# Narrower score windows in a neighbourhood-attention block: 23, 31 and 24 key columns, and value rows loaded in small pieces

## The chip, the cores and the metric

The kernel runs on one core of one Trainium2 chip. Its time is the device time of one execution in microseconds; the time before is the median of three runs. The engines are TensorE (PE, with PEld for its weight loads), VectorE (DVE), ScalarE (ACT), GpSimd (POOL) and SyncE (SP), whose only work here is to issue transfers. ACT issues a few transfers too.

## The reference

One encoder layer over 1024 tokens of 1024 channels. The normalised input goes through one projection. Half of its columns feed a gated convolution over 31 positions, the other half an attention with 8 heads of 64 channels. Both outputs are joined, projected and added to the input; then a gated feed-forward layer follows. The change touches the attention alone:

```
qg = q.reshape(B, rows, GRID_W, H, Dh)        # 16 rows of 64 tokens
col_start = jnp.clip(cols - kw // 2, 0, GRID_W - kw)      # kw = 16
row_start = jnp.clip(r - kh // 2, 0, rows - kh)           # kh = 8
s = jnp.einsum("bqhd,brqchd->bhqrc", q_r, k_win) * scale
s = s + bias                                   # learned, by 2-D offset
p = jax.nn.softmax(s, axis=(-2, -1))
out = jnp.einsum("bhqrc,brqchd->bqhd", p, v_win)
```

A query at row r and column c of the 16 by 64 grid sees 8 rows and 16 columns of keys around it, clamped to the grid.

## The kernel before, in words

The queries are cut in 8 tiles of 128: two halves of the grid's rows (`rh`, 8 rows each) by four blocks of 16 columns (`cb`). For a tile the kernel computes scores against a rectangle of keys that covers all its queries' windows, and a table of biases holds -1e30 where a query may not look. The rectangle has `AR` = 12 rows and, from `WIN`, 24, 32, 32 or 24 columns: 288 or 384 keys. `order` (line 667) takes the column blocks 0, 3, 1, 2, each with both halves: eight stages. A stage has four pairs of heads, numbered `i` = 0 to 31 over all stages.

For a pair: `score_mm` (line 680) makes two products of 64 rows by the rectangle; `score_max` (693) adds the table and finds the largest on DVE; `score_exp` (698) exponentiates on ACT and sums; `score_norm` (709) divides on POOL. `flip` (720) transposes the probabilities on PE in three groups of four key rows (96 or 128 keys each), `flip_out` (727 on DVE for even pairs, 729 on ACT for odd ones) copies them back, and `weigh` (739) multiplies them by the values, summing over three groups. Even pairs put scores and transposes into the same two PSUM banks (`cv`), one after the other.

The order of the work is written out by hand: engines run their instructions in the order of the program. The loop at line 880 takes two pairs a turn: scores of `i` and `i+1`, transposes of `i-3` and `i-2`, weighing of `i-5` and `i-4`. Before it, the value projection of tokens (`value`, eight steps of 128 tokens) is interleaved with the first pairs. `value_out` (447) stores each step's values to DRAM on ACT's queue.

Values come back from DRAM by `load_vw` (660) on SP's queue: for a window, tiles of two groups, a group being four grid rows; one load per grid row of the four, so a group lies as 4 x 24 or 4 x 32 rows of a tile, and two groups may come in one load. `load_vw(0, 0, 1)` and `load_vw(0, 2)` follow the seventh value step, `load_vw(0, 3)`, `load_window(3)` and a table the eighth; windows 1 and 2 are loaded in the loop. `table` (647) loads a stage's biases, made in DRAM far earlier by `bias_tables` (lines 510 to 527) with many small transfers, which share SP's queue with the weights' loads (149).

Tiles named G, ST, H are taken from rings of buffers; the framework places the waits. A transfer signals its landing by one of eight semaphores, dealt in turn over the transfers of both queues.

Of the kernel before, what the change touches and what calls it, by code (L numbers as in the profile page):

```python
# [6 lines left out]
F32 = mybir.dt.float32  # L7
# [5 lines left out]
P = 128  # L13
# [4 lines left out]
NH = 8  # L18
HD = 64
# [3 lines left out]
EPS = 1e-6  # L23
NEG = -1e30
GW = 64
AR = 12
SIDE = (16, 17, 18, 19, 20, 21, 22)
WIN = ((0, 24, 8), (8, 32, 0), (24, 32, 0), (40, 24, 0))


def layout(v):
# [39 lines left out]
def build(ctx, tc, a):  # L71
    nc = tc.nc
    pe, act, dve, pool = nc.tensor, nc.scalar, nc.vector, nc.gpsimd
# [45 lines left out]
    def lr(w):  # L119
        return w[:, :512], w[:, 512:]  # L120
# [127 lines left out]
    ident = T("ident", [P, P], 1, "ident")  # L248
# [24 lines left out]
    for _ in range(9):  # L273
# [4 lines left out]
    t1 = [dr.tile([NH, 16, 15, ncol], F32, name=f"t1{ty}") for ty, ncol in enumerate((24, 32, 24))]  # L278
    tf = {(rh, ty): dr.tile([16, 8, NH, AR * t1[ty].shape[-1]], F32, name=f"tf{rh}{ty}")
          for rh in range(2) for ty in range(3)}  # L280

    def rstd_of(ss, scale, name):
# [159 lines left out]
    vd = dr.tile([S, 512], F32, name="vd")  # L442
# [57 lines left out]


    aside_dma = []

    def bias_tables():
        neg = G("neg")
        pool.memset(neg, NEG)

        def fill1(ty):
            n = 15 * t1[ty].shape[-1]
            nc.sync.dma_start(t1[ty].rearrange("h j u b -> (h j) (u b)"), neg[:, :n])  # L510

        def fill2(rh, ty):
            n = 3 * AR * t1[ty].shape[-1] if ty != 1 else 2 * AR * 32
            for o in range(0, NH * AR * t1[ty].shape[-1], n):
                w = min(n, NH * AR * t1[ty].shape[-1] - o)
                nc.sync.dma_start(tf[rh, ty].rearrange("j i h c -> (j i) (h c)")[:, o:o + w], neg[:, :w])

        def run(ty, j):
            b0, shift = ((max(j - 8, 0), 15), (j, 7), (min(j, 8), 7))[ty]
            o = b0 - j + shift  # L520
            nc.sync.dma_start(t1[ty][:, j, :, b0:b0 + 16], a["rpb"][:, :, o:o + 16])

        def rows_of(rh, ty, i):
            ncol = t1[ty].shape[-1]
            a0 = max(i - 4, 0) if rh == 0 else min(i, 4)
            u0 = a0 - i + (7 if rh == 0 else 3)
            nc.sync.dma_start(tf[rh, ty][:, i, :, a0 * ncol:(a0 + 8) * ncol],
                              t1[ty][:, :, u0:u0 + 8, :].rearrange("h j u b -> j h (u b)"))
        for ty in (0, 2, 1):
            fill1(ty)  # L530
        for ty in (0, 2, 1):
            aside_dma.extend(lambda ty=ty, j=j: run(ty, j) for j in range(16))
            for rh in range(2):
                aside_dma.append(lambda rh=rh, ty=ty: fill2(rh, ty))
        for ty in (0, 2, 1):
            for rh in range(2):
                aside_dma.extend(lambda rh=rh, ty=ty, i=i: rows_of(rh, ty, i) for i in range(8))
# [30 lines left out]
    for kp in range(4):  # L568
        parts = []
# [66 lines left out]


    def table(rh, ty):
        n = AR * t1[ty].shape[-1]
        src = tf[rh, ty].rearrange("j i h c -> (j i) (h c)")  # L640
        if rh == 0 and ty == 0:
            parts = [(G(f"tab{k}")[:, :n * min(3, NH - 3 * k)], 3 * k) for k in range(3)]
        else:
            parts = [(H(f"tab{rh}{ty}")[:, :NH * n], 0)]
        heads = []
        for w, h0 in parts:
            nc.sync.dma_start(w, src[:, h0 * n:h0 * n + w.shape[-1]])
            heads += [w[:, o:o + n] for o in range(0, w.shape[-1], n)]
        return heads


    vwt, vw = {}, {}

    def load_vw(cb, *gs):
        c0, ncol, _ = WIN[cb]
        if gs[0] % 2 == 0:
            vwt[cb, gs[0] // 2] = G(f"vw{cb}{gs[0]}").rearrange("p (g d) -> p g d", d=512)
        w = vwt[cb, gs[0] // 2]
        for r in range(4):
            nc.sync.dma_start(w[r * ncol:(r + 1) * ncol, gs[0] % 2:gs[-1] % 2 + 1, :],  # L660
                              vd.rearrange("(g r c) d -> r c g d", r=4, c=GW)[r, c0:c0 + ncol, gs[0]:gs[-1] + 1, :])
        for g in gs:
            vw[cb, g] = w[:4 * ncol, g % 2, :]
# [5 lines left out]
    at = []  # L669

    def score_mm(i):
        s_, hp = divmod(i, 4)
        rh, cb = order[s_]
        t = rh * 4 + cb
        c0, ncol, _ = WIN[cb]
        s2 = cv(f"s{i}") if i > 0 and i % 2 == 0 else None
        out = []
        for hh in range(2):
            s = (mm(f"s{i}{hh}") if s2 is None else lr(s2)[hh])[:, :AR * ncol]
            pe.matmul(s, qT[hh * HD:(hh + 1) * HD, hp, t * P:(t + 1) * P],  # L680
                      k4[hh * HD:(hh + 1) * HD, hp, rh * 4:rh * 4 + AR, c0:c0 + ncol], start=True, stop=True)
# [28 lines left out]


    def flip(i):
        s_, hp = divmod(i, 4)
        m = 4 * WIN[order[s_][1]][1]
        if i % 2 == 0:
            cvs[i] = cv(f"p{i}")
        pp[i] = lr(cvs[i]) if i % 2 == 0 else [mm(f"p{i}{hh}") for hh in range(2)]
        for hh, pt in enumerate(pp[i]):
            for g in range(3):
                pe.transpose(pt[:m, g * P:(g + 1) * P], es[i][:, hh, g * m:(g + 1) * m], ident)  # L720

    def flip_out(i, hh=None):
        m = 4 * WIN[order[i // 4][1]][1]
        w = et[i][:m, :, :384]
        pTs[i] = [w[:, h].rearrange("p (n q) -> p n q", q=P) for h in range(2)]
        if hh is None:
            dve.tensor_copy(w, cvs[i].rearrange("p (h n) -> p h n", h=2)[:m, :, :384])
        else:
            act.copy(w[:, hh], pp[i][hh][:m, :384])

    def weigh(i):
        s_, hp = divmod(i, 4)
        rh, cb = order[s_]
        if hp == 0:
            os_[s_] = tp(f"o{s_}").rearrange("p (c q) -> p c q", c=4)
        for g in range(3):
            for hh in range(2):
                c = (2 * hp + hh) * HD
                pe.matmul(os_[s_][hh * HD:(hh + 1) * HD, hp], vw[cb, rh + g][:, c:c + HD], pTs[i][hh][:, g],  # L739
                          start=g == 0, stop=g == 2)  # L740

    def half(name):
        w = H(name, F32R).rearrange("p (w k s) -> p w k s", w=2, s=512)
# [21 lines left out]
    def load_window(cb):  # L765
        load_vw(cb, 0, 1)
        load_vw(cb, 2, 3)
# [112 lines left out]
    for i in range(4, 32, 2):  # L880
# [24 lines left out]
        if i > 4:  # L905
            weigh(i - 5)
# [541 lines left out]
    def quarter(w, o, t):  # L1448
        return w[:, o + t * 512:o + t * 512 + 512]
# [32 lines left out]
    for s, p in enumerate(SEQ):  # L1482
        for k in range(QF - 2):
            n = s * QF + k
# [23 lines left out]
    for half in range(2):  # L1508
# [4 lines left out]
        w = quarter(om["u"], 0, 3)[:, part_]  # L1513
# [17 lines left out]
```

## Time and profile before

| | us |
|---|---|
| median of three runs (1035.32 to 1035.88) | 1035.74 |
| the profiled execution | 1035.18 |
| its span, first to last instruction | 1033.5 |
| PE busy in the span | 1024.3 |
| DVE busy | 782.3 |
| ACT busy | 478.7 |
| POOL busy | 436.0 |
| attention loop, first scores to last weighing of the loop | 235.6 to 295.1 |
| TensorE clock granted | 1.0 throughout |

A row of the timeline gives start and length in us from the span's start, the engine (a q behind it means its queue or sequencer), the line of the kernel, what it writes and reads, the shapes, and how many instructions are merged in the row; in brackets stands the engine's idle time before it and what ended that. A wait row gives who waited for whom, the total in us, how often, and the longest. Matmul lengths overlap the next one's start, so times between starts are the ones to use.

### The profile page before, as it was taken

The page shows a single profiled execution, that of the slowest core. Times are in us where ns is not written, and L with a number is a line of the kernel's source. Part 1 is how long each engine was busy: PE and PEld are TensorE (multiplying, and loading weights), DVE is VectorE, ACT ScalarE, POOL GpSimd, SP SyncE. Part 2 cuts the span into 40 slices and gives each one's busy share as a digit, 9 for nine tenths or more (in the row PEclk, how much of TensorE's full clock was granted, in tenths as well). Part 3 has the DMA queues.
Part 4 walks back from the last instruction along what each step waited for, and adds up shares of the span by engine and source line. Part 5 has one row for each costly group of instructions (what it writes and reads, how often), then busy time and mean ns, then how long its engine had stood idle before and what let it go on. Part 6 is the DMA issues. An engine that isn't in the chain of part 4 may idle for free.

```text
span 1033.5 us, 15158 instructions
## 1 busy us (share of the span) xinstructions
PE 1024.3 (99%) x5334; PEld 853.8 (83%) x5334; DVE 782.3 (76%) x1234; ACT 478.7 (46%) x1045; POOL 436.0 (42%) x345
## 2 busy tenths in 40 slices
PE   9999999999999999999999999999999999999998
PEld 7888888877787788877888888888888888888887
DVE  5788997896755376998787787787787767758874
ACT  7565348836866345523334334343342443433432
POOL 1036764524641345047776667567566200003210
PEclk9999999999999999999999999999999999999999
DMA  9426781337403621122434424434441696633631
GB/s 347 165 79 201 225 255 53 122 115 234 124 22 122 235 92 41 47 107 89 156 119 157 139 96 153 153 101 145 144 143 71 222 365 238 224 102 123 214 122 42
DMA packets 75084, 152.53 MB, mean 148 GB/s; under 512 B 13824, under 2 KB 22784, under 8 KB 74368
## 3 DMA queue, kind: packets, MB, share of 16 engines
q1 hardware_dynamic: 72992, 148.21, 42.5%
q10 hardware_dynamic: 2016, 3.36, 0.9%
q8 instruction: 42, 0.69, 0.3%
q14 instruction: 34, 0.28, 0.1%
HBM read 112.38 MB, written 44.76 MB: 152 GB/s over the span
## 4 chain that ended last, share of the span: by engine, by line
PE 93%; DVE 5%; ACT 1%; issue 1%; DMA 0%; ACTq 0%; DVEq 0%
PE B L115 5%; PE B L116 5%; PE B L117 5%; PE z L115 4%; PE z L117 4%; PE z L116 4%; PE D L115 3%; PE D L116 3%; PE D L117 3%; PE gl L117 3%; PE gl L116 3%; PE gl L115 3%; PE pj L115 3%; PE pj L116 3%; PE pj L117 3%; PE p L720 2%
## 5 line engine op out<-in xcount | busy, mean ns | idle before, releaser
L363 DVE SCALAR_TENSOR_TENSOR cv<-u,par,cv 128x1009 f32<-128x1009 f32 (+14 forms) x92 | 117.4, 1277 | 2.3
L389 POOL TENSOR_TENSOR pa<-pa,pr 128x1022 f32<-128x1022 f32 (+5 forms) x24 | 58.0, 2417 | 48.7 <-ACT pr L388 36.1
L107 ACT CAST op<-sr 128x512 fp32r<-128x512 f32 x77 | 47.7, 619 | 57.7 <-PE B2d L117 26.7
L1474 POOL TENSOR_TENSOR ou<-ou,resm 128x512 f32<-128x512 f32 x8 | 12.0, 1506 | 139.8 <-DVE ou L1465 126.1
L111 DVE TENSOR_TENSOR op<-sr,op 128x512 fp32r<-128x512 f32 x77 | 57.6, 748 | 16.5 <-ACT op L107 16.4
L709 POOL TENSOR_SCALAR e<-e,rs 128x288 f32<-128x288 f32 (+1 forms) x64 | 33.9, 545 | 41.8 <-DVE rs L707 40.1
L1024 DVE TENSOR_TENSOR ts<-gu,ts 128x512 f32<-128x512 f32 x40 | 46.3, 1158 | 0.7
L107 ACT CAST op<-wd 128x512 fp32r<-128x512 f32 x54 | 33.4, 619 | 28.5 <-DVE wd L1370 18.0
L698 ACT ACTIVATE e<-e,mx 128x288 f32<-128x288 f32 (+1 forms) x64 | 36.5, 572 | 18.8 <-DVE mx L693 16.9
L111 DVE TENSOR_TENSOR op<-wd,op 128x512 fp32r<-128x512 f32 x54 | 39.8, 738 | 1.7 <-ACT op L107 0.6
L693 DVE CUSTOM_DVE_ANT_0 e<-s,tab 128x288 f32<-128x288 f32 (+1 forms) x64 | 28.7, 503 | 13.6 <-PE s L680 13.6
L980 POOL TENSOR_TENSOR sq<-sq,sq 128x512 f32<-128x512 f32 x12 | 17.1, 1423 | 51.6 <-ACT sq L976 51.4
L1283 DVE TENSOR_TENSOR g<-D,g 128x512 f32<-128x512 f32 x22 | 15.2, 690 | 23.4 <-PE D L117 23.4
L416 ACT ACTIVATE sq<-z,r 128x64 f32<-128x64 f32 x96 | 28.3, 329 | 5.2 <-PE z L117 5.2
L1260 ACT ACTIVATE D<-D 128x512 f32<-128x512 f32 x22 | 12.8, 582 | 32.6 <-DVE D L1259 32.6
L388 ACT ACTIVATE pr<-u,par 128x1022 f32<-128x1022 f32 (+5 forms) x24 | 27.0, 1138 | 1.6 <-ACT vs L446 1.2
L720 PEld LDWEIGHTS p<-ident,e 128*96 128x96 f32 (+1 forms) x192 | 20.5, 133 | 6.8 <-POOL e L709 6.3
L115 PE MATMUL B2d<-op 128*128 128x512 f32 x66 | 25.8, 391 | 0.0
L117 PE MATMUL B2d<-op 128*128 128x512 f32 x66 | 25.7, 389 | 0.0
L116 PE MATMUL B2d<-op 128*128 128x512 f32 x66 | 25.7, 389 | 0.0
L739 PE MATMUL o<-e,vw 96*64 96x128 f32 (+1 forms) x384 | 24.7, 277 | 0.0
L720 PE MATMUL p<-ident,e 128*96 128x128 f32 (+1 forms) x192 | 24.4, 276 | 0.0
(1454 smaller groups left out, 3734.5 us busy)
## 6 DMA issues: line engine op xcount, KB each, us to landing
gu<-in_gu SPq DMA_DIRECT2D x44, 512.0 KB
sr<-sd SPq DMA_DIRECT2D x77, 256.0 KB
sd<-sd SPq DMA_DIRECT2D x22, 512.0 KB
wd<-in_wd SPq DMA_DIRECT2D x36, 256.0 KB
sd<-g SPq DMA_DIRECT2D x33, 256.0 KB
x<-in_x SPq DMA_DIRECT2D x8, 512.0 KB
xT<-in_xp SPq DMA_DIRECT2D x8, 512.0 KB
xd<-xT SPq DMA_DIRECT2D x16, 256.0 KB
```

Of the source, the lines that this page charges most:

```text
L107: act.copy(hi, src)
L111: eng.tensor_tensor(*[w[..., sl] for w in (lo, src, hi.bitcast(F32))], OP.subtract)
L115: pe.matmul(acc, lh, rh, start=start, stop=False, skip_group_check=True)
L116: pe.matmul(acc, lh, rl, start=False, stop=False, skip_group_check=True)
L117: pe.matmul(acc, ll, rh, start=False, stop=stop, skip_group_check=True)
L363: dve.scalar_tensor_tensor(acc[:, o], uc[:, i], dwk[:, c, t:t + 1], acc[:, o], OP.mult, OP.add)
L389: pool.tensor_tensor(pa[:, o], pa[:, o], pr[:, o], OP.add)
L693: dve.tensor_tensor_reduce(out=es[i][:, hh], in0=s[hh], in1=tab[rh, cb][2 * hp + hh], scale=-1.0, scalar=3.0e38, op0=OP.add, op1=OP.min, a ...
L698: act.activation(e, e, AF.Exp, bias=mx.pop((i, hh)), scale=-1.0, accum_out=sums[i][:, hh:hh + 1])
L709: pool.tensor_scalar(es[i][:, hh], es[i][:, hh], rs[:, hh:hh + 1], 1.0, op0=OP.mult, op1=OP.mult)
L720: pe.transpose(pt[:m, g * P:(g + 1) * P], es[i][:, hh, g * m:(g + 1) * m], ident)
L1024: dve.tensor_tensor(o, l, r, OP.subtract)
```

## The change

The rectangle of keys is cut to what some query of the tile may see: 11 rows for the upper half, 12 for the lower; 23, 31, 31 and 24 columns. The eight stages are then 253, 276, 264, 288, 341, 372, 341 and 372 keys wide. `groups` cuts a stage's keys in groups: of 128 for the first stage, so there are two, and of four grid rows for the others, so there are three. `whole` rounds a group's rows up to a multiple of 32; a transpose then takes a few of the next group's keys with it, and behind the last group POOL zeroes the columns up to the end. The value tiles get rows of zeros in the same places, loaded from a small zero array `zd` in DRAM, which `bias_tables` fills with one store.

Values of the first stage get a tile of their own, `load_first`, in which the 253 keys lie one behind the other. `value_rows` loads a run of rows whole if its length is a multiple of 8, and in pieces of up to 16 otherwise. So a group of the windows with 23 or 31 columns takes 9 loads (8 pieces and the zero rows) instead of 4, the first stage's tile 23, and windows with 24 columns stay at 4. The tables of the first stage lie in two buffers instead of three, and the table `table(1, 2)` is loaded ahead of the values of window 3 instead of behind them.

```
-AR = 12
+AR = (11, 12)
-WIN = ((0, 24, 8), (8, 32, 0), (24, 32, 0), (40, 24, 0))
+WIN = ((0, 23), (8, 31), (24, 31), (40, 24))
+NCOL = (23, 31, 24)
...
+    zd = dr.tile([4, 2, 512], F32, name="zd")
     def bias_tables():
         neg = G("neg")
         pool.memset(neg, NEG)
+        zero = ST("zero")[:8]
+        pool.memset(zero, 0.0)
+        nc.sync.dma_start(zd.rearrange("p g d -> (p g) d"), zero)
...
+            parts = [(G(f"tab{k}")[:, :4 * n], 4 * k) for k in range(2)]
-            parts = [(G(f"tab{k}")[:, :n * min(3, NH - 3 * k)], 3 * k) for k in range(3)]
...
+    def value_rows(w, at_, g, src, n):
+        m = n if n % 8 == 0 else 16
+        for o in range(0, n, m):
+            e = min(n, o + m)
+            nc.sync.dma_start(w[at_ + o:at_ + e, g, :], src[o:e])
+
+    def whole(n):
+        return -(-n // 32) * 32
+
     def load_vw(cb, *gs):
...
         for r in range(4):
-            nc.sync.dma_start(w[r * ncol:(r + 1) * ncol, gs[0] % 2:gs[-1] % 2 + 1, :],
-                              vd.rearrange("(g r c) d -> r c g d", r=4, c=GW)[r, c0:c0 + ncol, gs[0]:gs[-1] + 1, :])
+            value_rows(w, r * ncol, slice(gs[0] % 2, gs[-1] % 2 + 1), v4[r, c0:c0 + ncol, gs[0]:gs[-1] + 1, :], ncol)
+        n = whole(4 * ncol)
+        if n > 4 * ncol:
+            nc.sync.dma_start(w[4 * ncol:n, gs[0] % 2:gs[-1] % 2 + 1, :], zd[:n - 4 * ncol, :len(gs), :])
+    def load_first():
+        c0, ncol = WIN[0]
+        w = vwt["first"] = G("vwf").rearrange("p (g d) -> p g d", d=512)
+        for r in range(AR[0]):
+            for g in range(2):
+                a0, a1 = max(r * ncol, g * P), min((r + 1) * ncol, g * P + P)
+                if a0 < a1:
+                    t = r * GW + c0 + a0 - r * ncol
+                    value_rows(w, a0 - g * P, g, vd[t:t + a1 - a0, :], a1 - a0)
+        n = AR[0] * ncol - P
+        nc.sync.dma_start(w[n:whole(n), 1, :], zd[:whole(n) - n, 0, :])
...
+    def groups(s_):
+        n, m = width(s_), P if s_ == 0 else 4 * WIN[order[s_][1]][1]
+        return [slice(o, min(o + m, n)) for o in range(0, n, m)]
...
-            es[i] = et[i][:, :, :AR * WIN[cb][1]]
+            n, gs = width(s_), groups(s_)
+            es[i] = et[i][:, :, :n]
+            end = gs[-1].start + whole(gs[0].stop)
+            if n < end:
+                pool.memset(et[i][:, :, n:end], 0.0)
...
-            for g in range(3):
-                pe.transpose(pt[:m, g * P:(g + 1) * P], es[i][:, hh, g * m:(g + 1) * m], ident)
+            gs = groups(i // 4)
+            m = whole(gs[0].stop)
+            for g, k in enumerate(gs):
+                pe.transpose(pt[:m, g * P:(g + 1) * P], et[i][:, hh, k.start:k.start + m], ident)
...
-                pe.matmul(os_[s_][hh * HD:(hh + 1) * HD, hp], vw[cb, rh + g][:, c:c + HD], pTs[i][hh][:, g],
-                          start=g == 0, stop=g == 2)
+                pe.matmul(os_[s_][hh * HD:(hh + 1) * HD, hp], v[:n, c:c + HD], pTs[i][hh][:n, g],
+                          start=g == 0, stop=g == len(gs) - 1)
...
     value(6)
-    load_vw(0, 0, 1)
+    load_first()
+    load_vw(0, 1)
     load_vw(0, 2)
...
     load_vw(0, 3)
+    tab[1, 3] = table(1, 2)
     load_window(3)
-    tab[1, 3] = table(1, 2)
```

More of the change, by code (lines that the diff above doesn't have):

```diff
@@ L277, in build @@
     qgs = T("qgs", [P, 1], 1, "qgs")
-    t1 = [dr.tile([NH, 16, 15, ncol], F32, name=f"t1{ty}") for ty, ncol in enumerate((24, 32, 24))]
-    tf = {(rh, ty): dr.tile([16, 8, NH, AR * t1[ty].shape[-1]], F32, name=f"tf{rh}{ty}")
+    t1 = [dr.tile([NH, 16, 15, ncol], F32, name=f"t1{ty}") for ty, ncol in enumerate(NCOL)]
+    tf = {(rh, ty): dr.tile([16, 8, NH, AR[rh] * NCOL[ty]], F32, name=f"tf{rh}{ty}")
           for rh in range(2) for ty in range(3)}
@@ L506, in bias_tables @@
         pool.memset(neg, NEG)
+        zero = ST("zero")[:8]
+        pool.memset(zero, 0.0)
+        nc.sync.dma_start(zd.rearrange("p g d -> (p g) d"), zero)
         def fill1(ty):
-            n = 15 * t1[ty].shape[-1]
+            n = 15 * NCOL[ty]
             nc.sync.dma_start(t1[ty].rearrange("h j u b -> (h j) (u b)"), neg[:, :n])
         def fill2(rh, ty):
-            n = 3 * AR * t1[ty].shape[-1] if ty != 1 else 2 * AR * 32
-            for o in range(0, NH * AR * t1[ty].shape[-1], n):
-                w = min(n, NH * AR * t1[ty].shape[-1] - o)
+            n = (3 if ty != 1 else 2) * AR[rh] * NCOL[ty]
+            for o in range(0, NH * AR[rh] * NCOL[ty], n):
+                w = min(n, NH * AR[rh] * NCOL[ty] - o)
                 nc.sync.dma_start(tf[rh, ty].rearrange("j i h c -> (j i) (h c)")[:, o:o + w], neg[:, :w])
@@ L523, in rows_of @@
         def rows_of(rh, ty, i):
-            ncol = t1[ty].shape[-1]
+            ncol = NCOL[ty]
             a0 = max(i - 4, 0) if rh == 0 else min(i, 4)
@@ L652, in build @@
     vwt, vw = {}, {}
+    def value_rows(w, at_, g, src, n):
[5 more added lines that the diff above has]
+        return -(-n // 32) * 32
     def load_vw(cb, *gs):
-        c0, ncol, _ = WIN[cb]
-        if gs[0] % 2 == 0:
+        c0, ncol = WIN[cb]
+        if (cb, gs[0] // 2) not in vwt:
             vwt[cb, gs[0] // 2] = G(f"vw{cb}{gs[0]}").rearrange("p (g d) -> p g d", d=512)
         w = vwt[cb, gs[0] // 2]
+        v4 = vd.rearrange("(g r c) d -> r c g d", r=4, c=GW)
         for r in range(4):
-            nc.sync.dma_start(w[r * ncol:(r + 1) * ncol, gs[0] % 2:gs[-1] % 2 + 1, :],
-                              vd.rearrange("(g r c) d -> r c g d", r=4, c=GW)[r, c0:c0 + ncol, gs[0]:gs[-1] + 1, :])
+            value_rows(w, r * ncol, slice(gs[0] % 2, gs[-1] % 2 + 1), v4[r, c0:c0 + ncol, gs[0]:gs[-1] + 1, :], ncol)
+        n = whole(4 * ncol)
+        if n > 4 * ncol:
+            nc.sync.dma_start(w[4 * ncol:n, gs[0] % 2:gs[-1] % 2 + 1, :], zd[:n - 4 * ncol, :len(gs), :])
         for g in gs:
-            vw[cb, g] = w[:4 * ncol, g % 2, :]
+            vw[cb, g] = w[:, g % 2, :]
+    def load_first():
[9 more added lines that the diff above has]
+        nc.sync.dma_start(w[n:whole(n), 1, :], zd[:whole(n) - n, 0, :])
     k4 = kT.rearrange("p c (r w) -> p c r w", w=GW)
@@ L669, in build, with width @@
     at = []
+    def width(s_):
+        rh, cb = order[s_]
+        return AR[rh] * WIN[cb][1]
+    def groups(s_):
+        n, m = width(s_), P if s_ == 0 else 4 * WIN[order[s_][1]][1]
+        return [slice(o, min(o + m, n)) for o in range(0, n, m)]
     def score_mm(i):
@@ L674, in score_mm @@
         t = rh * 4 + cb
-        c0, ncol, _ = WIN[cb]
+        c0, ncol = WIN[cb]
         s2 = cv(f"s{i}") if i > 0 and i % 2 == 0 else None
@@ L678, in score_mm @@
         for hh in range(2):
-            s = (mm(f"s{i}{hh}") if s2 is None else lr(s2)[hh])[:, :AR * ncol]
+            s = (mm(f"s{i}{hh}") if s2 is None else lr(s2)[hh])[:, :width(s_)]
             pe.matmul(s, qT[hh * HD:(hh + 1) * HD, hp, t * P:(t + 1) * P],
-                      k4[hh * HD:(hh + 1) * HD, hp, rh * 4:rh * 4 + AR, c0:c0 + ncol], start=True, stop=True)
+                      k4[hh * HD:(hh + 1) * HD, hp, rh * 4:rh * 4 + AR[rh], c0:c0 + ncol], start=True, stop=True)
             out.append(s)
@@ L712, in flip @@
     def flip(i):
-        s_, hp = divmod(i, 4)
-        m = 4 * WIN[order[s_][1]][1]
         if i % 2 == 0:
@@ L718, in flip @@
         for hh, pt in enumerate(pp[i]):
-            for g in range(3):
-                pe.transpose(pt[:m, g * P:(g + 1) * P], es[i][:, hh, g * m:(g + 1) * m], ident)
+            gs = groups(i // 4)
+            m = whole(gs[0].stop)
+            for g, k in enumerate(gs):
+                pe.transpose(pt[:m, g * P:(g + 1) * P], et[i][:, hh, k.start:k.start + m], ident)
     def flip_out(i, hh=None):
-        m = 4 * WIN[order[i // 4][1]][1]
-        w = et[i][:m, :, :384]
+        gs = groups(i // 4)
+        m, n = whole(gs[0].stop), len(gs) * P
+        w = et[i][:m, :, :n]
         pTs[i] = [w[:, h].rearrange("p (n q) -> p n q", q=P) for h in range(2)]
         if hh is None:
-            dve.tensor_copy(w, cvs[i].rearrange("p (h n) -> p h n", h=2)[:m, :, :384])
+            dve.tensor_copy(w, cvs[i].rearrange("p (h n) -> p h n", h=2)[:m, :, :n])
         else:
-            act.copy(w[:, hh], pp[i][hh][:m, :384])
+            act.copy(w[:, hh], pp[i][hh][:m, :n])
     def weigh(i):
@@ L735, in weigh @@
             os_[s_] = tp(f"o{s_}").rearrange("p (c q) -> p c q", c=4)
-        for g in range(3):
+        gs = groups(s_)
+        for g, k in enumerate(gs):
+            n = whole(k.stop - k.start)
+            v = vwt["first"][:, g, :] if s_ == 0 else vw[cb, rh + g]
             for hh in range(2):
                 c = (2 * hp + hh) * HD
-                pe.matmul(os_[s_][hh * HD:(hh + 1) * HD, hp], vw[cb, rh + g][:, c:c + HD], pTs[i][hh][:, g],
-                          start=g == 0, stop=g == 2)
+                pe.matmul(os_[s_][hh * HD:(hh + 1) * HD, hp], v[:n, c:c + HD], pTs[i][hh][:n, g],
+                          start=g == 0, stop=g == len(gs) - 1)
     def half(name):
```

2 lines of the change are left out of this document (1 added, 1 removed).

## The prediction

> **What bounds the kernel now.** I read the page first: the busy shares and the chain that ended last. The columns of the first row are busy time, share and instructions.
>
> ```profile
> PE 1024.3 (99%) x5334; PEld 853.8 (83%) x5334; DVE 782.3 (76%) x1234; ACT 478.7 (46%) x1045; POOL 436.0 (42%) x345
> ...
> PE 93%; DVE 5%; ACT 1%; issue 1%; DMA 0%; ACTq 0%; DVEq 0%
> ```
>
> PE sets the end, but an average over 1033.5 us says nothing of the attention stage that the change edits. So I took the timeline of PE there; columns are start, length, engine, line, and in brackets the idle time before and what ended it. An fp32 product is two entries, a transpose is one.
>
> ```profile
> 235.64 1.24 PE L680 MATMUL s<-kT,qT 64*128 64x288 f32 x8
> 236.82 1.51 PE L720 MATMUL p<-ident,e 128*96 128x128 f32 x12
> 238.26 0.88 PE L739 MATMUL o<-e,vw 96*64 96x128 f32 x12
> 239.45 1.24 PE L680 MATMUL s<-kT,qT 64*128 64x288 f32 x8 [0.31 <-DVE e L727]
> ...
> 243.52 1.24 PE L680 MATMUL s<-kT,qT 64*128 64x288 f32 x8
> 244.69 1.52 PE L720 MATMUL p<-ident,e 128*96 128x128 f32 x12
> 246.14 1.53 PE L739 MATMUL o<-e,vw 96*64 96x128 f32 x24
> 247.60 1.24 PE L680 MATMUL s<-kT,qT 64*128 64x288 f32 x8
> ...
> 251.68 1.24 PE L680 MATMUL s<-kT,qT 64*128 64x288 f32 x8
> ...
> 259.83 1.56 PE L680 MATMUL s<-kT,qT 64*128 64x384 f32 x8
> 261.33 1.51 PE L720 MATMUL p<-ident,e 128*96 128x128 f32 x12
> ...
> 274.54 1.53 PE L720 MATMUL p<-ident,e 128*128 128x128 f32 x12
> 275.99 1.53 PE L739 MATMUL o<-e,vw 128*64 128x128 f32 x24
> 277.45 1.56 PE L680 MATMUL s<-kT,qT 64*128 64x384 f32 x8
> ```
>
> One turn of the loop (two pairs of heads) is scores, transposes, weighing, then the next scores with no gap: 243.52 to 247.60 is 4.08 us of PE and nothing else. Only the first turn shows a gap, 0.31 us before 239.45, for the copy of line 727 that frees the two banks which scores and transposes share. That gap says how near the second limit is: 3.81 us from 235.64 to 239.45 is the shortest turn which that copy allows, 0.27 under 4.08. So PE time saved here is worth its full size only for the first quarter of a microsecond in a turn.
>
> **What the change saves on PE.** Key columns fall from 24 to 23 and 32 to 31, rows from 12 to 11 for the upper half of the queries. Widths of the eight stages in their order: 288, 288, 288, 288, 384, 384, 384, 384 become 253, 276, 264, 288, 341, 372, 341, 372: 35+12+24+0+43+12+43+12 = 181 columns, times 8 heads = 1448. The score block of four products starts the transposes 1.17 us later at 288 columns (243.52 to 244.69) and 1.50 at 384 (259.83 to 261.33): 0.33 us for 4x96 columns, 0.86 ns each. 1448 x 0.86 ns = 1.24 us.
>
> [...]
>
> The first stage, 253 wide, is cut in two groups of 128 and 125 instead of three of 96: one transpose and one weighing product fewer for each of 8 heads. A transpose costs 1.45/12 = 0.121 us (244.69 to 246.14): 8 x 0.121 = 0.97. A weighing product costs 1.46/12 = 0.122 (246.14 to 247.60): 0.97. The groups elsewhere stay three, their sums still run over 96 or 128 rows, so the padding to 32 costs PE nothing: with 128 rows the transposes take 1.45 us (274.54 to 275.99) and the weighing 1.46 (to 277.45), as with 96. Together 3.18 us; in the first two turns the copy's limit gives back about 0.3 (the second turn's PE work falls by 0.77, its limit by about 0.5). **PE: -2.85 us.** Of this 2.05 lies before the fifth pair's weighing, which matters below.
>
> **What it adds off PE, at no cost.** 28 memsets on POOL that zero the ends of the probabilities. Nearest row and the work beside it:
>
> ```profile
> L384 POOL MEMSET pa<- x4: 98/114/123, 33.3 to 182.6; 128x1 f32 x4
> ...
> 59.88 0.96 POOL L506 MEMSET neg<- 128x1024 f32 x1
> ...
> 242.02 0.98 POOL L709 TENSOR_SCALAR e<-e,rs 128x288 f32<-128x288 f32 x2 [1.41 <-DVE rs L707]
> ```
>
> Two a turn at 0.12 us, up to 0.2 for 35 columns, stand ahead of the normalisation in POOL's queue, and POOL idles 1.41 us there waiting for DVE. If that cover went, at most 0.4 us a turn. DVE and ACT get less work (fewer columns); neither sets the turn after the second. A zero tile and its store join SP's queue ahead of the bias fills, which start right after the 0.96 us memset: half a memset (0.5) and an issue (0.4) push all that follows by 0.9 us. The nearest user is the last weight of the query projection:
>
> ```profile
> 140.08 2.85 POOL L111 TENSOR_TENSOR w03l<-w03r,w03h 128x1024 fp32r<-128x1024 f32 x1
> ...
> 144.91 0.39 PE L116 MATMUL z<-w03l,hT 128*128 128x512 f32 x1
> ```
>
> It is ready at 142.93 and wanted at 144.91: 2.0 us of slack against 0.9. Nothing. The tables of the bias shrink a little. More waits stand in PE's queue at the weighing (more loads per tile); the present ones leave no gap at 246.14, so I take 0.
>
> **The value loads.** This part decides. Before, the values of the first window come in 12 loads; now the first stage's own tile takes 23 (22 pieces of 7 to 16 rows and a row of zeros), and three more groups 9 each: 50. Call the stores of value tokens (line 447, on ACT's queue) t0 to t7. First SP's queue and ACT's stores:
>
> ```profile
> 210.13 0.75 SPq L660 DMA_DIRECT2D vw<-vd  x2
> 217.59 0.71 SPq L660 DMA_DIRECT2D vw<-vd  x2
> 229.68 0.29 SPq L660 DMA_DIRECT2D vw<-vd  x1
> 230.01 1.50 SPq L660 DMA_DIRECT2D vw<-vd  x3
> 238.52 1.53 SPq L660 DMA_DIRECT2D vw<-vd  x4
> 239.68 2.85 SPq L660 DMA_DIRECT2D vw<-vd  x7
> 242.57 1.30 SPq L647 DMA_DIRECT2D tab<-tf  x3
> ...
> 227.66 0.33 ACTq L447 DMA_DIRECT2D vd<-vs  x1
> 228.76 0.33 ACTq L447 DMA_DIRECT2D vd<-vs  x1
> 236.47 0.33 ACTq L447 DMA_DIRECT2D vd<-vs  x1
> ```
>
> The store t5 (227.66) frees a load at 229.68, t7 (236.47) at 238.52: 2.05 us from issue to landing. From 238.52 ten loads go out before 242.57 (the fourth of one row is the first of the next): 0.405 us each, 48 KB or 96 KB alike. Now the other limit:
>
> ```profile
> 249.80 0.30 SPq L660 DMA_DIRECT2D vw<-vd  x1
> 253.52 0.30 SPq L660 DMA_DIRECT2D vw<-vd  x1
> 259.62 0.30 SPq L660 DMA_DIRECT2D vw<-vd  x1
> ...
> SPq L660 <- DMA vd<-vs: 24.1, 4, 10.5
> SPq L660 <- DMA tab<-tf: 11.4, 3, 5.8
> ```
>
> After the three tables at 242.57 to 243.49 five value loads follow, then SP stands still three times for a table landing, though no value load reads a table. A transfer waits for the landing of the eighth before it: the framework deals eight completion semaphores in turn, over SP's loads and ACT's stores together. That is the trap: a value load dealt the semaphore of t7 cannot go before 238.52, whatever it reads.
>
> What is wanted when: the first weighing at 238.26 minus 0.5 (its tile: loads 1 to 23), the fifth pair's weighing, which reads the three other groups (24 to 50), at 246.14 + 0.73 - 2.05 = 244.8.
>
> Bound below: no load waits for another's semaphore. After 229.68 there remain 30 loads (those that read t5 and later): 30 x 0.405 + 2.05 puts the last landing at 243.9, 0.9 before 244.8. No stall: cost 0. Bound above: t7 is dealt after ten value loads, as it is now (two, four and four issue ahead of 238.52). Then the 18th and all behind it wait: 33 loads from 238.52, the last issued 32 x 0.405 later, landing 253.5: a stall of 8.7 us. I take fifteen ahead of t7: more than ten, since a piece is a third of a load and the queue gets further, but not double, since each issue costs the same. Then the 23rd waits (the zero row of the first tile, so the first weighing stalls at 237.8 to 240.6 already) and 28 loads go from 238.52: last issue 27 x 0.405 later = 249.5, landing 251.5. **Stall 6.7 us**, all before the fifth pair's weighing, the first part included. The table for the fourth stage is moved ahead of the next window's loads in SP's queue and behind these 50: issued near 250, it is wanted some 6 us after 251.5; the first of three tables took 242.57 to 249.80, 7.2 us, beside two others, and it has fewer beside it, so 0, up to 1. The two later windows take 18 loads each instead of 8: 20 more x 0.405 = 8 us of SP, wanted from 276 on. Nothing.
>
> [...]
>
> **Sum**, against the profiled execution's own 1035.18: -2.85 + 6.7 = 1039.0. The median of the runs is 1035.74, 0.56 above that execution: 1039.6.
>
> **Rivals.**
> 1. The loads are hidden: t7 is dealt behind 32 or more loads, or the stores do not block. For it: the bound below leaves 0.9 us. Against it: the queue now gets ten loads out by then. Time 1035.74 - 2.85 = 1032.9, faster. The point from which it decides: each load further ahead of t7 takes 0.405 off the stall, which ends at 32 (8.7/0.405 = 21.5 past ten).
> 2. Half hidden: 20 to 30 loads ahead. Stall 4.7 to 0.6, time 1037.6 to 1033.5, mostly within 0.2%.
> 3. A store waits for a late load: ACT's queue then stands with the exponentials behind it, and PE with them. For it: both queues share the semaphores. Against it: eight loads before t7 go out early. It adds about 2 us: 1041.6.
> 4. Small transfers at a higher price each. By the longest issue spacing in a crowded queue that the rows show between loads of one tile, 1.5/3 = 0.5 us (230.01), 28 loads take 2.6 us more: 1042.2. [...]
>
> **How the numbers follow.** Forecast (11 to 19 loads ahead, 1037.9 to 1041.2) 0.45; rival 1 0.22; rival 2 0.20; rival 3 0.08; rival 4 0.05. 0.2% is 2.07 us, about what this kernel's runs can tell. Slower by more: forecast, 3 and 4: 0.58; rival 2 gives 0.18 to no change and 0.02 to faster: 0.24 faster, 0.18 the same. Range: from rival 1 to the upper bound, 1035.74 - 2.85 - 0.2 = 1032.7 to 1035.74 - 2.85 + 8.7 + 0.4 = 1042.0; the likeliest case's own is 1037.9 to 1041.2.
>
> **What would show it.** Scores at 276 columns and weighing rows x16 for the first stage show the PE terms; turns of 4.0 us outside the stalls. A gap of PE before line 739's successor, ended by a DMA of vw from vd, in the first weighing or the fifth pair's, with SP's value loads still issuing near 248, shows the stall; if PE runs through there and SP is done by 243, rival 1 holds. A long gap on ACT before its store shows rival 3. I am wrong most easily in the count ahead of t7, which I cannot read from the kernel before.

## The result, and the profile after

The changed kernel takes 1032.79 us (median; 1032.24 to 1033.33), the kernel before, on the same chip, 1035.67: a ratio of 0.9972, 95% interval 0.9961 to 0.9983. It is faster, by 2.9 us. I had forecast 1039.6 and slower; what came is rival 1, the hidden loads, at 1032.9. The profiled execution took 1032.93 us with a span of 1031.2, against 1035.18 and 1033.5.

The page of the kernel after, its first row (busy time, share, instructions) and the chain that ended last:

```profile
PE 1022.9 (99%) x5310; PEld 853.3 (83%) x5310; DVE 780.5 (76%) x1234; ACT 478.3 (46%) x1045; POOL 436.6 (42%) x374
...
PE 93%; DVE 5%; ACT 1%; issue 1%; POOL 0%; DVEq 0%; ACTq 0%; POOLq 0%
```

PE is still the bound. It has 24 instructions fewer on the page (8 transposes, and 8 weighing products of two entries), and POOL has its 28 memsets and one more. The timeline of PE in the same place as before (start, length, engine, line, tiles and shapes, count; in brackets idle time and what ended it):

```profile
235.80 1.20 PE L716 MATMUL s<-kT,qT 64*128 64x276 f32 x8
236.94 1.25 PE L760 MATMUL p<-ident,e 128*128 128x128 f32 x8
238.11 0.80 PE L783 MATMUL o<-e,vwf 128*64 128x128 f32 x8
239.03 1.20 PE L716 MATMUL s<-kT,qT 64*128 64x276 f32 x8
...
242.73 1.16 PE L716 MATMUL s<-kT,qT 64*128 64x264 f32 x8
243.82 1.51 PE L760 MATMUL p<-ident,e 128*96 128x128 f32 x12
245.27 0.66 PE L783 MATMUL o<-e,vwf 128*64 128x128 f32 x8
245.75 0.83 PE L783 MATMUL o<-e,vw 96*64 96x128 f32 x12
246.51 1.16 PE L716 MATMUL s<-kT,qT 64*128 64x264 f32 x8
...
250.51 1.24 PE L716 MATMUL s<-kT,qT 64*128 64x288 f32 x8
```

No row has a bracket: PE never waits, neither in the first weighing (238.11) nor in the fifth pair's (245.75), where I had put a stall. The turns last 3.23, 3.70, 3.78 and 4.00 us, where before they lasted 3.81, 4.07, 4.08 and 4.08. The gap of 0.31 us behind the first weighing is gone too. Now SP's queue and ACT's last store:

```profile
230.91 0.27 SPq L692 DMA_DIRECT2D vwf<-zd  x1
231.28 2.77 SPq L663 DMA_DIRECT2D vw<-vd  x8
...
234.49 2.78 SPq L663 DMA_DIRECT2D vw<-vd  x8
...
237.65 2.98 SPq L663 DMA_DIRECT2D vw<-vd  x8
240.67 0.29 SPq L678 DMA_DIRECT2D vw<-zd  x1
241.07 0.35 SPq L652 DMA_DIRECT2D tab<-tf  x1
```

```profile
235.91 0.69 ACT L447 ACTIVATE vs<-z,r 128x512 f32<-128x512 f32 x1 [3.05 <-PE z L118]
236.93 0.33 ACTq L448 DMA_DIRECT2D vd<-vs  x1
237.31 0.53 ACT L738 ACTIVATE e<-e,mx 128x276 f32<-128x276 f32 x1 [0.71 <-DVE mx L733]
```

The queue stands for t7 (stored at 236.93) for only some 0.2 us: the first load that reads it, a piece of grid row 14, leaves at 239.26, 0.56 behind the load before it instead of 0.35. From 230.91 to 240.67 it sends 27 loads in 9.76 us, 0.36 each, and its last load leaves 5.1 us before the products of the fifth pair that want this window's values. The trace's records also name the semaphore that each transfer signals:

```
start   transfer                   semaphore
235.19  load, third of group 2     104
235.55  load                       105
...
237.31  load, zeros of group 2      99
237.65  load, first of group 3     101
236.93  store t7 (on ACT's queue)  104
238.00  load, second of group 3    105
```

t7 was dealt its semaphore behind 42 value loads. The next load with the same semaphore is the last of the fifty, at 240.67, and by the same records t7 has landed at 239.24. So the 0.2 us above are a wait for t7's data, and nothing waits for its semaphore alone. (The store itself waits a little, 236.60 to 236.93, for the load of 235.19.)

### The profile page after: what moved, and what is told of

Its sections match the earlier page's. It is cut to its first block, busy times and chain, and to the rows that moved or that the text cites. A ratio compares the mean times of both kernels' runs of the same rounds, so it can differ in the third digit from the quotient of the medians.

```text
span 1031.2 us, 15232 instructions
## 1 busy us (share of the span) xinstructions
PE 1022.9 (99%) x5310; PEld 853.3 (83%) x5310; DVE 780.5 (76%) x1234; ACT 478.3 (46%) x1045; POOL 436.6 (42%) x374
## 4 chain that ended last, share of the span: by engine, by line
PE 93%; DVE 5%; ACT 1%; issue 1%; POOL 0%; DVEq 0%; ACTq 0%; POOLq 0%
PE B L116 5%; PE B L117 5%; PE B L118 5%; PE z L116 4%; PE z L118 4%; PE z L117 4%; PE D L116 3%; PE D L117 3%; PE D L118 3%; PE gl L118 3%; PE gl L116 3%; PE gl L117 3%; PE pj L116 3%; PE pj L117 3%; PE pj L118 3%; PE p L760 2%
## 5 line engine op out<-in xcount | busy, mean ns | idle before, releaser
L749 POOL TENSOR_SCALAR e<-e,rs 128x341 f32<-128x341 f32 (+5 forms) x64 | 33.1, 531 | 38.3 <-DVE rs L747 37.3
L738 ACT ACTIVATE e<-e,mx 128x341 f32<-128x341 f32 (+5 forms) x64 | 35.4, 555 | 18.0 <-DVE mx L733 15.0
L733 DVE CUSTOM_DVE_ANT_0 e<-s,tab 128x341 f32<-128x341 f32 (+5 forms) x64 | 27.2, 481 | 12.9 <-PE s L716 12.9
L760 PEld LDWEIGHTS p<-ident,e 128*128 128x128 f32 (+1 forms) x184 | 19.7, 135 | 6.7 <-POOL e L749 5.1
L760 PE MATMUL p<-ident,e 128*128 128x128 f32 (+1 forms) x184 | 23.9, 277 | 0.0
L915 DVE TENSOR_TENSOR xT<-pj,xT 128x512 f32<-128x512 f32 x16 | 10.8, 684 | 16.5 <-PE pj L118 16.5
```

The source lines that it names most:

```text
L738: act.activation(e, e, AF.Exp, bias=mx.pop((i, hh)), scale=-1.0, accum_out=sums[i][:, hh:hh + 1])
L749: pool.tensor_scalar(es[i][:, hh], es[i][:, hh], rs[:, hh:hh + 1], 1.0, op0=OP.mult, op1=OP.mult)
L760: pe.transpose(pt[:m, g * P:(g + 1) * P], et[i][:, hh, k.start:k.start + m], ident)
```

## The experiments

All start from the kernel after. The kernel before, on the same chip, took 1035.4 to 1035.9 us beside them. "Against after" below is the difference of two distances to the kernel before.

**How far t7 stands back.** Three kernels change nothing but the order of the first window's value loads, so that more of them go out behind t7's landing: 19, 23 and 32 instead of 5 (eight by the order of dealing).

```
     value(6)
     load_first()
-    load_vw(0, 1)
-    load_vw(0, 2)
 ...
     value(7)
     flip_out(0)
     step()
     load_vw(0, 3)                       # reads t7
+    load_vw(0, 1)
+    load_vw(0, 2)                       # late: 23 behind t7
```

`behind18`, run last of the three, leaves 4 of group 1's nine loads ahead; `later` also moves the last four of the first tile's eleven rows of keys behind group 3. In these kernels SP's queue stands because group 3 reads t7, not because of a semaphore; what follows the landing is the same.

> A smaller stall of the same kind as the first run with reordered groups: 4 of group 1's nine loads stay ahead of group 3, so 19 loads instead of 23 go out behind t7. There the last left at 246.78 and PE went on at 248.51. Here the last leaves 4 x 0.353 earlier, at 245.4, and lands 1.73 later, at 247.1; the third group of products is wanted at 245.84: a gap of 1.3 us. Theory A (a gap costs its own length): 1032.8 + 1.3 = 1034.1. Theory B (behind any gap PE runs at half clock for a time, as behind the gap of 2.67, where 5.1 us of products took about 2.5 more): 1036.0 to 1036.6. [...]

> The three groups of the first window's values are loaded in the order 3, 1, 2 instead of 1, 2, 3, behind the first stage's tile. Group 3 reads t7, so 23 loads go out only after t7 has landed. Theory A (a stall is the last landing minus the moment it is wanted, at 0.353 us a load, as the trace after shows from 230.20 to 240.67): t7's store leaves at 236.93 and lands 2.05 later, at 239.0; the last of 23 loads leaves 22 x 0.353 after 239.1, at 246.9, and lands at 248.9; the fifth pair's third group of products is wanted near 246.0. Stall 2.9 us, time 1032.8 + 2.9 = 1035.7. Theory B (the issue price is the 0.405 of the prediction): 250.1, stall 4.1, time 1036.9. Theory C (late value loads are hidden by something else): 1032.8.

> As my forecast supposed: t7 is dealt behind 18 value loads, with 32 behind it. The first 14 loads of the first stage's tile stay, then come group 3 (which reads t7), the other 9 loads of that tile, groups 1 and 2. Theory A (0.353 us a load): the first tile's last load is the 14th from 239.1, leaves at 243.7, lands at 245.7; the first weighing's second group is wanted at 238.4: stall 7.3 us. The last of 32 leaves at 250.0 and lands at 252.1, when the fifth pair's products are wanted only at 246.0 + 7.3 = 253.3: no more. Time 1032.8 + 7.3 = 1040.1. Theory B (0.405): first tile at 246.4, stall 8.0, and the last landing 253.7 against 254.0: time 1040.8. Theory C (hidden): 1032.8.

| | loads behind t7's landing | us | ratio to before (95%) | against after | PE's gap |
|---|---|---|---|---|---|
| after | 5 | 1032.79 | 0.9972 (0.9961 to 0.9983) | | none |
| behind18 | 19 | 1035.03 | 0.9996 (0.9986 to 1.0005) | +2.3 | 1.21, 0.52 |
| late | 23 | 1038.30 | 1.0024 (1.0014 to 1.0035) | +5.6 | 2.67 |
| later | 32 | 1040.17 | 1.0048 (1.0033 to 1.0063) | +7.5 | 6.31 |

PE's timeline in the three, in that order:

```profile
247.25 0.66 PE L785 MATMUL o<-e,vw 96*64 96x128 f32 x8 [1.21 <-DMA vw<-zd]
247.84 1.16 PE L718 MATMUL s<-kT,qT 64*128 64x264 f32 x8
...
256.29 0.44 PE L785 MATMUL o<-e,vw 96*64 96x128 f32 x4 [0.52 <-DMA vw<-vd]
```

```profile
248.51 1.12 PE L783 MATMUL o<-e,vw 96*64 96x128 f32 x8 [2.67 <-DMA vw<-vd]
249.56 2.13 PE L716 MATMUL s<-kT,qT 64*128 64x264 f32 x8
251.63 2.79 PE L760 MATMUL p<-ident,e 128*96 128x128 f32 x12
```

```profile
244.52 0.69 PE L787 MATMUL o<-e,vwf 128*64 128x128 f32 x4 [6.31 <-DMA vwf<-zd]
245.14 2.21 PE L720 MATMUL s<-kT,qT 64*128 64x276 f32 x8
247.28 1.66 PE L764 MATMUL p<-ident,e 128*128 128x128 f32 x10
```

Loads that go out behind t7's landing do stall PE, in the two places that the prediction named, and the more of them, the longer: the gaps came out a little under those worked out (1.3, 2.9, 7.3). But the price of a gap is not its length. In the second kernel the scores behind it take 2.13 us instead of 1.16 and the transposes 2.79 instead of 1.51. The table by stretches shows why; its columns are the stretch, its length, PE busy and count, granted clock, DMA share, GB/s; the 19-load kernel first, then the 23-load and the 32-load one:

```profile
246.00:250.00 4.00, 2.79 (x28) 1.00 0.84 282
```

```profile
246.00:250.00 4.00, 1.49 (x10) 0.74 0.60 167
250.00:254.00 4.00, 4.00 (x19) 0.50 0.86 277
254.00:258.00 4.00, 4.00 (x42) 0.91 1.04 281
...
0.00:1036.50 1036.50, 1025.45 (x5310) 1.00 0.44 146
```

```profile
238.00:244.00 6.00, 0.21 (x4) 0.77 0.23 50
244.00:248.00 4.00, 3.48 (x16) 0.50 0.29 61
248.00:252.00 4.00, 3.91 (x40) 1.00 0.47 95
```

Behind the gap of 2.67 us the granted clock is half (0.50 from 250 to 254); behind the one of 1.21 it stays whole (1.00 from 246 to 250). PE's time over the whole span says the same: 1025.45 us in the 23-load kernel, 2.6 above the 1022.9 of after, on top of the 2.67 of the gap. The price also differs from run to run: the eight runs of the 23-load kernel spread from 1036.65 to 1039.34. The 19-load kernel has the 1.21 and a second gap of 0.52, for the next window's values, and its PE time is that of after (1022.88).

**What the small pieces are for.** One number of `value_rows` is changed.

```
-        m = n if n % 8 == 0 else 16
+        m = n if n % 8 == 0 else 8        # pieces8; likewise 6, 13, 17
+        m = n                             # onepiece
```

> Each run of 23, 31 or fewer rows is loaded whole: 5 loads a group instead of 9, 13 for the first stage's tile instead of 23. Theory A (loads are hidden and only their number costs queue time): no change, 1032.8, the queue done near 235 up to the group that reads t7. Theory B (a load of 23 rows is much slower than two small ones, more than 3.3 us longer to land): a stall of its excess over 3.3 us, time over 1033.5.

> Pieces of up to 17 rows instead of 16: 23 rows are 17 + 6, 31 are 17 + 14; the number of loads stays the same. [...] Theory B (the price goes by the bytes and number of loads): 1032.8.

> Pieces of up to 13 rows: 23 rows are 13 + 10, 31 are 13 + 13 + 5; in the first window as many loads as after. [...] Theory B (only multiples of 8 or 16 rows are fast): as slow as the pieces of 17 rows or the whole runs, 1038 or more.

> Runs of rows that are no multiple of 8 are loaded in pieces of up to 8 rows instead of 16: 13 loads a group instead of 9. Behind t5 stand 43 loads instead of 30. Theory A: from 230.20 the last leaves 42 x 0.353 later, at 245.0, and lands at 247.1, wanted near 246.0: stall 1.1 us, time 1033.9. Theory B (0.405 a load): 249.3, stall 3.3, time 1036.1. Theory C: hidden, 1032.8.

> The same in pieces of up to 6 rows: 17 loads a group, 56 behind t5. Theory A: the last leaves at 230.2 + 55 x 0.353 = 249.6, lands at 251.7, stall 5.7 us, time 1038.5; the difference to pieces of 8 is 13 loads x 0.353 = 4.6 us. Theory B (0.405): 254.5, stall 8.5, time 1041.3. Theory C: 1032.8.

| rows in a piece | loads of 23 and 31 rows are | us | ratio to before (95%) |
|---|---|---|---|
| up to 6 | 6+6+6+5, 5x6+1 | 1055.21 | 1.0197 (1.0180 to 1.0214) |
| up to 8 | 8+8+7, 8+8+8+7 | 1037.89 | 1.0024 (1.0015 to 1.0034) |
| up to 13 | 13+10, 13+13+5 | 1032.81 | 0.9973 (0.9962 to 0.9984) |
| up to 16 (after) | 16+7, 16+15 | 1032.79 | 0.9972 (0.9961 to 0.9983) |
| up to 17 | 17+6, 17+14 | 1067.48 | 1.0305 (1.0288 to 1.0322) |
| whole | 23, 31 | 1107.34 | 1.0689 (1.0674 to 1.0704) |

A row more than 16 costs 35 us, which theory B there had at nothing; 13 rows, no multiple of 8, cost nothing. Pieces of 6 lose far more than I expected (1038.5), but not because each is dearer: in the first window they leave 0.34 us apart (16 from 237.15 to 242.52), where pieces of 16 leave 0.36 apart. It is their number. t7's store waits for one of them, ACT stands 9.61 us behind the store, and PE waits for ACT:

```profile
247.12 2.72 PE L760 MATMUL p<-ident,e 128*128 128x128 f32 x10 [6.91 <-ACT e L770]
```

A second gap, 7.1 us between 274 and 300, is for the values of a window of 31 columns, and the clock falls at both (0.53 from 243 to 250, 0.80 from 274 to 300). In the kernel with whole runs SP's queue and PE's waits (who for whom, us in total, times, longest) are:

```profile
283.04 5.13 SPq L678 DMA_DIRECT2D vw<-zd  x1
288.21 15.54 SPq L663 DMA_DIRECT2D vw<-vd  x4
303.79 5.12 SPq L678 DMA_DIRECT2D vw<-zd  x1
```

```profile
PE o L783 <- DMA vw<-vd: 41.0, 2, 21.8
PE o L783 <- DMA vw<-zd: 16.1, 3, 7.2
PE p L760 <- ACT e L770: 7.2, 1, 7.2
```

The table by stretches, over the whole span (length, PE busy and count, granted clock, DMA share, GB/s):

```profile
0.00:1106.10 1106.10, 1033.00 (x5310) 0.97 0.41 137
```

A run of 31 rows of two groups, 124 KB, holds the queue for some 5.13 us: 24.7 GB/s. The zero rows, a small load, wait as long, since their issue stands behind it. Of the 74.9 us between the spans (1106.1 and 1031.2) 10.1 is PE's own time at a lowered clock (1033.00 against 1022.86), 64.8 is idle. The pieces of 17 rows show the same in SP's queue: a group of a 31-column window, in eight loads of 17 and 14 rows, takes 11.69 us (273.68 to 285.37), where eight of 16 and 15 rows take 3.46 (265.49 to 268.95, after) and twelve of 13, 13 and 5 take 5.34 (261.54 to 266.88). With pieces of up to 17 rows PE waits 20.8 us for value loads, in four waits, the longest 11.4; with up to 16 the profile has no such wait, with up to 13 none of 0.4 us or more. What sets loads of 17, 23 and 31 rows apart from those of 16, 15, 13, 10 and 7 is not shown: the profile has no row by DMA engine, and the records of the semaphores in after say only that a load of 16 rows raises its semaphore 16 times and loads of 13, 10 and 7 rows 14, 11 and 8 times.

With pieces of 8 rows the loss is not the late landing that I had expected (1.1 us), but this, in ACT and then PE:

```profile
236.17 0.69 ACT L447 ACTIVATE vs<-z,r 128x512 f32<-128x512 f32 x1 [3.05 <-PE z L118]
241.19 0.33 ACTq L448 DMA_DIRECT2D vd<-vs  x1
241.56 0.52 ACT L738 ACTIVATE e<-e,mx 128x276 f32<-128x276 f32 x1 [4.70 <-DMA vw<-vd]
```

```profile
243.08 2.71 PE L760 MATMUL p<-ident,e 128*128 128x128 f32 x10 [2.59 <-ACT e L770]
```

That is rival 3 of the prediction. t7's store is dealt the semaphore of a value load, the queue runs later than it was planned, and the store waits for that load with ACT's exponentials behind it: 4.70 us of ACT, a gap of 2.59 in PE and a lowered clock behind that (0.61 from 242 to 246). (PE stands another 1.09 us up to 276.78, for the values of a window of 31 columns.) To test it, the store was taken off ACT's queue:

```
-        nc.scalar.dma_start(vd[t * P:(t + 1) * P, :], vs)
+        if t < 7:
+            nc.scalar.dma_start(vd[t * P:(t + 1) * P, :], vs)
+        else:
+            for o in range(0, P, 32):
+                nc.gpsimd.dma_start(vd[t * P + o:t * P + o + 32, :], vs[o:o + 32])
```

> Pieces of 8 rows again, but the eighth value step's store (t7) is issued as four stores of 32 rows on POOL's queue, whose transfers signal by semaphores of their own. Theory A (with pieces of 8, ACT stood 4.70 us only because t7's store waited for the semaphore of a value load issued late): ACT's exponentials come at 237.3 as after, PE's gap of 2.59 at the transposes is gone, and the fifth pair's products wait instead, for the last load, which left at 247.19 and lands 1.73 later at 248.9, against 246.0 wanted: a gap of 2.9 us there, a lowered clock behind it, and 1037 to 1039 in all. Theory B (ACT stood for another reason): the gap at the transposes stays.

It took 1039.60 us (ratio 1.0034, 1.0020 to 1.0048). ACT, POOL and PE:

```profile
236.79 0.53 ACT L742 ACTIVATE e<-e,mx 128x276 f32<-128x276 f32 x1 [0.54 <-DVE mx L737]
```

```profile
236.56 0.69 POOL L452 DMA_DIRECT2D vd<-vs  x1 [2.84 <-ACT vs L447]
239.09 0.52 POOL L452 DMA_DIRECT2D vd<-vs  x1 [1.84 <-issue]
241.39 0.51 POOL L452 DMA_DIRECT2D vd<-vs  x1 [1.78 <-issue]
243.60 0.50 POOL L452 DMA_DIRECT2D vd<-vs  x1 [1.71 <-issue]
```

```profile
244.75 2.43 PE L764 MATMUL p<-ident,e 128*128 128x128 f32 x10 [4.87 <-POOL e L753]
```

ACT no longer stands (0.54 us instead of 4.70), so the store's wait was its cause. But the remedy costs more than the harm: each store takes POOL 2.2 to 2.5 us to issue, and the normalisation stands behind four of them. PE's gap has stayed at the transposes, with POOL to blame instead of ACT, so the gap of 2.9 us that I expected at the fifth pair could not appear.

**The two PE terms.** The first stage goes back to three groups.

```
-        n, m = width(s_), P if s_ == 0 else 4 * WIN[order[s_][1]][1]
+        n, m = width(s_), 4 * WIN[order[s_][1]][1]
 ...
-    load_first()
+    load_vw(0, 0)
```

> The first stage goes back to three groups of four grid rows (92 keys, 96 rows with the zeros) like the other stages, and its values to the tiles of the other groups; widths stay 253 to 372. So 8 transposes and 8 weighing products come back. Theory A (the first two turns are bound by PE now): 8 x 0.121 + 8 x 0.122 = 1.94 us, time 1032.8 + 1.9 = 1034.7, and what is left against the kernel before, about 1.0 to 1.2, is the 1448 columns at 0.86 ns. Theory B (the copy of the transposed probabilities bounds those turns, as the gap of 0.31 before suggested): 1.0 to 1.6, time 1033.8 to 1034.4. Theory C (the gain is elsewhere): 1032.8.

1033.94 us, ratio 0.9985 (0.9976 to 0.9994): 1.5 us under before. That is what is left of the change without the two groups, in the main the 1448 columns (1.24 by the prediction, within the interval). The kernel without padding below, run beside it and equal to after in PE's work, took 1032.48; so the two groups are worth 1.46 (1.64 predicted: 1.94 less 0.3). With three groups the gap of the copy is back, to the hundredth:

```profile
239.97 1.20 PE L716 MATMUL s<-kT,qT 64*128 64x276 f32 x8 [0.31 <-DVE e L768]
```

**The padding to 32 rows.**

```
     def whole(n):
-        return -(-n // 32) * 32
+        return n
 ...
-        n = AR[0] * ncol - P
-        nc.sync.dma_start(w[n:whole(n), 1, :], zd[:whole(n) - n, 0, :])
```

> Sums run over the 92, 93, 96, 124 or 125 rows that hold keys, not over multiples of 32, and the zero rows of the value tiles and their loads are gone; the output is the same. Theory A (PE's price is that of moving columns; the trace shows the same 1.46 us for 96 and for 128 rows): no change, 1032.8 within 0.5. Theory B (a sum over a number of rows that is no multiple of 32 is dearer): slower, by the count of such products, 8 x 20 of 0.122 us each, up to 20 us if their price doubled.

1032.48 us, ratio 0.9970 (0.9958 to 0.9981). A sum over 92 rows costs what one over 96 costs:

```profile
249.08 1.53 PE L781 MATMUL o<-e,vw 92*64 92x128 f32 x24
...
257.24 1.54 PE L781 MATMUL o<-e,vw 96*64 96x128 f32 x24
```

So the rounding to 32 and the loads of zero rows bought no time and cost none.

**The memsets.** Each was issued four times.

```
-                pool.memset(et[i][:, :, n:end], 0.0)
+                for _ in range(4):
+                    pool.memset(et[i][:, :, n:end], 0.0)
```

> Each of the 28 memsets that zero the ends of the probabilities is issued four times. Theory A (POOL's wait for the reciprocals, 1.2 to 1.3 us a turn, covers them): six more of about 0.1 us in a turn, 0.6 us, cost nothing: 1032.8. Theory B (they push the normalisation and with it the transposes): up to 0.6 us in 14 turns less the cover, 1033 to 1036.

1032.85 us, ratio 0.9973 (0.9962 to 0.9983): no cost. The timeline of POOL with four, and of after, shows the cover being used up, 1.47 us where a wait of 1.20 stood:

```profile
243.75 1.47 POOL L731 MEMSET e<- 128x48 f32 x8
245.19 0.96 POOL L750 TENSOR_SCALAR e<-e,rs 128x276 f32<-128x276 f32 x2
```

```profile
243.75 0.21 POOL L730 MEMSET e<- 128x48 f32 x2
245.16 0.97 POOL L749 TENSOR_SCALAR e<-e,rs 128x276 f32<-128x276 f32 x2 [1.20 <-DVE rs L747]
```

**The moved table.**

```
+    load_window(3)
     tab[1, 3] = table(1, 2)
-    load_window(3)
```

> The table of the fourth stage is loaded behind the eight loads of the next window, as before, not ahead of them. After, it left at 241.07, and the eighth transfer behind it waited until 247.25 for its semaphore, so it took about 6.1 us. Theory A: it leaves some 3.5 to 4 us later (eight loads of 0.4 to 0.5), lands near 251, and the fourth stage's first scores come out at 251.3: 0 to 0.5 us, time 1032.8 to 1033.3. Theory B (the loads of the next window stop for t7 or a buffer until 247.25 whatever stands ahead): it lands near 253.5, stall 2, time 1034.8.

1032.94 us, ratio 0.9973 (0.9962 to 0.9984): not to be told from after. The trace shows the expected wait, first DVE's, then PE's:

```profile
252.34 0.46 DVE L733 CUSTOM_DVE_ANT_0 e<-s,tab 128x288 f32<-128x288 f32 x1 [1.35 <-PE s L716]
...
253.33 0.83 PE L760 MATMUL p<-ident,e 128*96 128x128 f32 x6 [0.64 <-DVE mx L733]
```

After, that DVE row came 1.0 us earlier (251.31, behind a wait of 0.47). The profile names the scores as what ended the wait, but they began at 250.66 here and at 250.51 after; what came later is the table, the only thing moved: it leaves at 244.71 here, the first of three, and left at 241.07 after, where by the semaphore records it landed at 247.23. PE stands 0.64 us; against the kernel without padding, timed beside it, the loss is 0.46, below what the runs can tell.

## Why the prediction was wrong

**The step that failed** is "I take fifteen ahead of t7". It was 42. I read "ten" off the kernel before and scaled it by the queue's speed. But those ten were all of the twelve loads that do not read t7: the data, not the time, had set the number. The same reading of the kernel after gives 45 of 50 (all but the four pieces of grid rows 14 and 15, and the zero rows behind them), and a stall of nothing by the prediction's own point of decision, 32. So the forecast's 0.45 should have gone to rival 1. Why the framework dealt t7 behind 42 and not behind all 45, no run shows. What was right is the size of a stall, once loads do go out behind t7: with 32 behind its landing (I had put 28) the time is 1040.17, against the 1039.6 forecast. That the two are so close is in part luck: the gap there stands in the first weighing, the fifth pair's comes for free behind it, and some of the loss is the clock, which the sum did not have. Nor is the trap itself shown, a load that stands for t7's semaphore alone: no load in these runs waited for t7 other than for its data.

**PE, -2.85 us**: right in its terms, a little large in size. The runs give 1.5 against 1.24 for the columns and 1.46 against 1.64 for the two groups; neither is told apart from its estimate. The rows are finer. From the first scores to the first product behind the loop the kernel before takes 74.39 us (220.71 to 295.10), the one after 71.89 (221.34 to 293.23) and the one with three groups 73.24 (221.48 to 294.72): 2.50 less in all, 1.15 for the columns and 1.35 for the groups. A transpose left out was worth less than the mean of the twelve, by which I had priced it: in the loop's first turn four fewer took 0.27 us off (1.44 to 1.17), not 0.48. So that the time meets rival 1's 1032.9 to 0.1 us is in part luck. For the columns the interval of the runs is 0.6 to 2.5, and the rows narrow it: in the kernel with the table moved back, the blocks of 264 and of 341 columns last 1.09 us (246.66 to 247.75) and 1.35 (259.63 to 260.98) from the scores to the transposes, 0.26 for 4 x 77 columns, 0.84 ns each against the 0.86 of the prediction.

**The price of a load, 0.405 us and 2.05 to land**: too dear. It was 0.36, and in the 23-load kernel PE went on 1.73 us after the last load left (246.78 to 248.51). The slack at the fifth pair is so about 3.4 us (240.67 + 1.73 to 245.75), not 0.9.

**POOL, the zero store, the padding: nothing**: right for the memsets and the padding, each by its own run; the store into the zero array was not tried alone. **The table: "0, up to 1"**: right that the move costs nothing, but the sum had no term for what it saves; left in its old place it would have come 1.0 us late and stopped PE for 0.64.

**Rival 3** did not happen (t7's store waited 0.3 us), but pieces half as long bring it about; I priced it at 2 us, and the run has 2.59 of gap, the lowered clock behind it, and the 1.09 later. **Rival 4** did not happen either: small loads were not dearer but cheaper than assumed (0.36 us each against 0.405), and it is the larger ones, of 17, 23 or 31 rows, that lose 35 to 75 us.

**A term that the sum lacked**: the clock behind a stall. 2.67 us of gap cost 5.6. The gaps of 1.21 us and less came without it.

## What to carry to other kernels

When a count is read from a trace to be carried over, first ask what ended it: ten loads were ahead of the store because the other two read it, not because there was no time for more. Time a load at the row count that it will have: here 17, 23 and 31 rows lost 35 to 75 us, and cut in pieces of 16, 15, 13, 10 and 7 rows they lost nothing. Each piece costs its issue, 0.34 to 0.36 us here, and a semaphore that some store may be waiting for. And a wait of PE is to be priced at its length plus what is left of a stretch at half clock when PE goes on; 2.59 us was enough for one here, 1.21 was not.

## What the hardware showed that was not expected

- 17 rows against 16 in a load: 35 us of the whole kernel (1067.48 against 1032.79); 31 rows whole: 124 KB in 5.13 us.
- The clock fell to half at gaps of PE of 2.59, 2.67, 4.87 and 6.31 us; it stayed whole behind 1.21. The stretch at half clock cost 2.6 us of PE time behind 2.67, but only about 1.2 behind 6.31 (2.21 for scores that take 1.20, 1.66 for transposes that take 1.45). The tables by stretches show why. With the clock taken as whole or half they give, as an estimate, a stretch of some 6.8 us behind both gaps, which begins while PE still stands: with 23 loads from about 247.9 to 254.7, and PE is back at 248.51; with 32 loads from about 241.2 to 248.0, and PE is back only at 244.52. Other stretches come out at about 3.4 us (behind 2.59) and 10.2 (with pieces of 6, behind 6.91). What decides the length, the runs do not settle.
- Stores of 32 rows on POOL's queue took POOL 2.2 to 2.5 us each (236.56 to 239.09 to 241.39 to 243.60).
